# Down projection's token operands split one unit behind their activations, stored as high and low halves; weight buffers shared by two products; accumulators loaded ahead

## The chip, the cores and the metric

The kernel runs on one core of a Trainium2 chip. A core has five engines that run side by side, each with its own queue of instructions: PE (TensorE, the matrix engine; its weight loads are a row of their own, PEld), DVE (VectorE), ACT (ScalarE), POOL (GpSimd) and SP (SyncE). Here SP issues all the DMAs that this text speaks of, one after the other. The engines' operands lie in SBUF (128 partitions); matmuls add up in banks of PSUM (the kernel has eight, named m).

The metric is the time of one execution in device microseconds. The kernel before took 2537.41 us, the median of three runs (2534.61 to 2539.2).

## The reference

One step of a streaming encoder with a single layer, in fp32: 512 new frames of one stream with 16 learned tokens ahead of them, and 64 frames of another stream with a cache.

```python
def trunk_layer(x, ...):
    h = rmsnorm(x, norm_attn_g)
    ...                                    # projections, two kinds of attention
    x = x + mix @ w_out
    h = rmsnorm(x, norm_ffn_g)
    x = x + (silu(h @ ffn_w_gate) * (h @ ffn_w_up)) @ ffn_w_down
    return x, ...
y_prompt = rmsnorm(xp[:, N_META:], final_norm_g)
y_sample = rmsnorm(xs, final_norm_g)
```

The width D_MODEL is 2048 and the FFN's width D_FF is 5632. In the FFN the kernel holds 576 tokens (TQ = 576, in two halves of QH = 288).

## The kernel before

**fp32 out of three matmuls.** Every fp32 operand is split into a high half, an ACT copy rounded to fp32r, and a low half, the DVE subtraction of that from the source. A product is then three matmuls: high x high, high x low, low x high. For weights the halves are wh and wl, for tokens bh and bl.

**Seven products instead of eight.** The FFN works on 2 x 2 blocks. `winograd` (L1068 to L1134) runs over seven products p; the token side of a product is one of seven combinations of four quarters (11, 12, 21, 22), the weight side one of seven combinations of raw weight blocks. Weight combinations are sums (ws) made on POOL (L1095) or DVE. For each product it splits the weights (`split_weights`), runs 2n matmuls with wh (L1126) and n with wl (L1130), each 128x128 by 128x288, and hands the bank to `take`, which copies (ACT) or adds (DVE) it into the result. Then it calls `step()`, by which other work is put behind that product in program order.

**Gate and up projection** (L1280 to L1329, about 1000 to 1962 us). 22 units u, each a gate set ("g") and an up set ("u") of seven products with n = 8, so 24 matmuls a product. Raw weights (raw, 1 MB each) come in by DMA. `gated` (L1268) multiplies the gate result by the token norm and applies silu; then POOL multiplies the up result by it (L1315) and forms four sums of quarters (L1321 to L1324) in the gate result's buffer. The results c go to HBM as actspill (two stores a unit), the sums as sumspill.

**Down projection** (L1426 to L1455, about 1970 to 2447 us). The 22 units of activations are taken in blocks of [4, 4, 4, 4, 4, 2]. Five blocks run `down_rows` (L1358): for each of eight pairs of output column blocks d, one `winograd` with n = 4, that is 7 x 12 matmuls, added into the accumulators y0 to y15 by DVE. Token operands of the next block are built meanwhile: `builder` (L1228) loads a quarter or a sum from actspill or sumspill (144 KB) four ahead, and a call of `step` issues half of its split (bh on ACT, bl on DVE, in place). For the first block this starts behind the third product of the last up set. In all 148 operands are split like this. wh and wl have two buffers each. The accumulators start as the residual and are loaded (x2spill) a pair at a time during the first block.

**Last block** (L1338, L1372 to L1424). Two units remain; `plain_rows` multiplies them without the seven products (L205), per half of the tokens, `squares` sums up for the norm, and `finish` transposes on PE (L1394), scales into output tiles (ot, four buffers) and stores.

**What sets the order.** Instructions go through a scheduler that orders each engine's queue; PE runs in program order, `pin` (from the down projection on) keeps the split in program order, and Q is the queue of loads and stores on SP. A new pool of buffers can be used once the buffers of the one that lay there are done: the pools of the gate and up stage are closed, and yy and yp opened, ahead of the down projection.

```python
    CHAIN = ((1, "a"), (5, "b"), (6, "a"), (2, "c"), (7, "a"), (3, "b"), (4, "a"))
    WIDE = ((1, "a"), (2, "c"), (4, "d"), (5, "b"), (6, "a"), (3, "b"), (7, "a"))
```

These are the orders of the products with their banks: CHAIN in the down projection and the last up set, WIDE elsewhere.

Of the kernel before, what the change touches and what calls it, by code (L numbers as in the profile page):

```python
# [2 lines left out]

# [128 lines left out]
def encoder_step(  # L132
# [196 lines left out]
    sumspill = dp.tile([FC // 2, P, 4, QH], F32, name="sumspill")  # L329
    mspill = dp.tile([KC, P, TQ], F32, name="mspill")  # L330
# [673 lines left out]
    rb2 = rw.tile([P, TQ], F32, name="rb2")  # L1004
    sq2 = rw.tile([P, TQ], F32, name="sq2")
# [13 lines left out]

    def operand(m, p, src):  # L1020
        hi = bc.tile([P, QH], F32R, name=f"bh{p}_{m}")
        lo = bc.tile([P, QH], F32R, name=f"bl{p}_{m}")
        pin(S.activation(hi, src, AF.Copy))
        pin(V.tensor_tensor(lo, src, f32(hi), op=ALU.subtract))
        operands[m, p] = (hi, lo)
# [41 lines left out]

    def winograd(wpool, spool, raws, slots, take, banks=None, engine=V, step=lambda: None, stag=("ws", 3),  # L1068
# [117 lines left out]
    close_ma()  # L1186
    fb, close_fb = pool("fb", "right")


    def stile():  # L1190
        return fr.tile([P, QH], F32, name="s", tag="s", bufs=4)

    def combined(c11, c12, c21, c22, chain):
# [15 lines left out]
        def take(p, banks):  # L1209
            if p == 1:  # L1210
                s[1] = stile()
                S.activation(s[1], banks[1], AF.Copy)
            elif p == 6:
                s[2] = stile()
# [13 lines left out]
    def builder(m0, count, plain, ahead, by_product=False):  # L1228

        srcs = {}  # L1230
        for m in range(m0, m0 + count):
            quarter = [actspill[2 * m + f, :, c] for f in range(2) for c in (slice(0, QH), slice(QH, TQ))]
            if plain:
                for p, src in zip((1, 2, 4, 5), quarter):
                    srcs[m, p] = src
            else:
                for p, src in zip(ORDER, (quarter[0], quarter[2], sumspill[m, :, 2], sumspill[m, :, 0],
                                          sumspill[m, :, 1], quarter[3], sumspill[m, :, 3])):
                    srcs[m, p] = src
        order = [p for p, _ in CHAIN]  # L1240
        todo = sorted(srcs, key=lambda mp: order.index(mp[1])) if by_product else list(srcs)

        def fetch(n):
            for m, p in todo[n:n + 1]:
                hi = bc.tile([P, QH], F32R, name=f"bh{p}_{m % 8}")
                lo = bc.tile([P, QH], F32R, name=f"bl{p}_{m % 8}")
                load(f32(lo), srcs[m, p])
                operands[m % 8, p] = (hi, lo)

        for n in range(ahead):  # L1250
            fetch(n)
        for n, (m, p) in enumerate(todo):
            fetch(n + ahead)
            hi, lo = operands[m % 8, p]
            pin(S.activation(hi, f32(lo), AF.Copy))
            yield
            pin(V.tensor_tensor(lo, f32(lo), f32(hi), op=ALU.subtract))
            yield
# [17 lines left out]

    turn = 0
    norm = token_norm()
    start = builder(0, blocks[0], False, 4, True)
    for u in range(FC // 2):  # L1280
        out = {}
        for which, wsrc in (("g", w_gate), ("u", w_up)):
# [9 lines left out]
            take = combined(*quarters(c[:, 0, :], c[:, 1, :]), chain)  # L1292
            done = [0]

            def step():
                if u == 0 and which == "u":
                    next(norm, None)
                if u == FC // 2 - 1 and which == "u":
                    done[0] += 1
                    if done[0] > 2:  # L1300
                        for _ in range(2 * blocks[0]):
                            next(start, None)
# [23 lines left out]
    for _ in start:  # L1326
        pass
# [206 lines left out]
```

## Time and profile before

| what | us |
|---|---|
| median of 3 runs | 2537.41 (2534.61 to 2539.2) |
| the profiled execution | 2533.22 |
| its span in the trace | 2531.3 |
| PE busy in the span | 2440.7 (96%) |
| DVE busy in the span | 1800.2 (71%) |
| ACT, POOL busy | 1106.6 (44%), 744.3 (29%) |

The span runs from the first to the last instruction of one profiled execution; 1.9 us of that execution lie outside it. In the rows of groups of instructions, `out<-in` names the tiles, `x824` is the count, then follow busy us, mean ns of one, and the engine's idle us ahead of them with what ended it. A busy PE is not PE at full rate: matmuls are pipelined, so the number of matmuls in a stretch says more than the busy share. A row of the windows has the stretch, then busy us and count for PE, PEld, DVE, ACT and POOL, then the clock that TensorE was granted, the DMA engines' busy share, and GB/s. A row of the timeline has start and length in us, with the idle time ahead in brackets. From the page of before:

```profile
PE   8999999989999999999999999999999899999997
...
DVE  5555555556555568877777777777777899999975
```

These are the busy tenths in 40 slices of 63.3 us: DVE's busiest stretch are the slices of the down projection, 32 to 38.

### The profile page before, as it was taken

Reading aid. Unit: us, or ns where it says so; the run is one execution under the profiler, and the core shown is the slowest. Engines: PE = TensorE matmul, PEld = TensorE weight load, DVE = VectorE, ACT = ScalarE, POOL = GpSimd, SP = SyncE. Lnnn points to the kernel's source line nnn. Section 1 sums busy time; section 2 is a strip of 40 time slices with the busy share of each in tenths; the row PEclk is TensorE's granted clock in tenths of the full one; section 3 lists DMA queues with packets and bytes.
Section 4 is the critical chain, followed back from the end, with each engine's and each line's share of the span. In section 5 each row is a group of like instructions: output and inputs, shape, how many; then the busy total and the mean of one; then the engine's idle time right before and its main releaser. Section 6 shows DMA issues by size and latency. Waiting matters only on the chain. (4 is left out here: it accounts for less than half of the span.)

```text
span 2531.3 us, 44872 instructions
## 1 busy us (share of the span) xinstructions
PE 2440.7 (96%) x17847; PEld 2381.8 (94%) x17847; DVE 1800.2 (71%) x2826; ACT 1106.6 (44%) x2008; POOL 744.3 (29%) x621
## 2 busy tenths in 40 slices
PE   8999999989999999999999999999999899999997
PEld 6999999988999888999999999999999899999997
DVE  5555555556555568877777777777777899999975
ACT  5343333333433444444444444444445444444445
POOL 0000000010000265644545454454543222222236
PEclk9999999999999999999999999999999899999999
DMA  7432232334322553333433333333335642542334
GB/s 216 141 93 80 81 87 83 82 111 120 100 84 76 166 151 112 125 126 121 137 109 117 117 125 132 119 125 100 128 128 167 207 150 84 159 157 84 111 100 150
DMA packets 330116, 307.73 MB, mean 122 GB/s; under 512 B 24708, under 2 KB 298507, under 8 KB 329907
## 3 DMA queue, kind: packets, MB, share of 16 engines
q1 hardware_dynamic: 329346, 302.80, 38.3%
q8 instruction: 140, 2.29, 0.4%
q0 software_dynamic: 560, 2.06, 0.2%
q14 instruction: 70, 0.57, 0.1%
HBM read 250.82 MB, written 56.68 MB: 121 GB/s over the span
## 5 line engine op out<-in xcount | busy, mean ns | idle before, releaser
L1126 PE MATMUL m<-bh,wh 128*128 128x288 f32 x3584 | 968.0, 296 | 11.0 <-DMA bl<-sumspill 8.4
L1126 PE MATMUL m<-bl,wh 128*128 128x288 f32 x3584 | 967.5, 295 | 0.0
L1126 PEld LDWEIGHTS m<-bh,wh 128*128 128x128 f32 x3584 | 673.9, 188 | 11.8 <-ACT wh L125 11.7
L1126 PEld LDWEIGHTS m<-bl,wh 128*128 128x128 f32 x3584 | 677.4, 189 | 0.1
L1130 PE MATMUL m<-bh,wl 128*128 128x288 f32 x3584 | 585.5, 298 | 17.1 <-DVE wl L125 14.5
L1130 PEld LDWEIGHTS m<-bh,wl 128*128 128x128 f32 x3584 | 512.2, 188 | 30.6 <-DVE wl L125 30.1
L1095 POOL TENSOR_TENSOR ws<-raw 128x512 f32<-128x512 f32 x256 | 344.1, 1352 | 599.1 <-DVE wl L125 319.2
L125 ACT ACTIVATE wh<-ws 128x512 fp32r<-128x512 f32 (+1 forms) x340 | 288.8, 849 | 447.6 <-PE m L1126 296.8
L125 DVE TENSOR_TENSOR wl<-ws,wh 128x512 fp32r<-128x512 f32 (+1 forms) x340 | 378.8, 1114 | 114.3 <-ACT wh L125 114.3
L125 DVE TENSOR_TENSOR wl<-raw,wh 128x512 fp32r<-128x512 f32 x416 | 403.7, 984 | 26.1 <-ACT wh L125 16.8
L125 ACT ACTIVATE wh<-raw 128x512 fp32r<-128x512 f32 x416 | 249.7, 626 | 306.2 <-PE m L1126 279.9
L108 PE MATMUL ps<-xh,wh 128*128 128x296 f32 x960 | 221.4, 312 | 1.2 <-ACT wh L125 1.2
L108 PE MATMUL ps<-xh,wl 128*128 128x296 f32 x960 | 210.7, 301 | 1.2 <-DVE wl L125 1.2
L108 PE MATMUL ps<-xl,wh 128*128 128x296 f32 x960 | 210.5, 301 | 0.0
L108 PEld LDWEIGHTS ps<-xh,wh 128*128 128x128 f32 x960 | 157.1, 191 | 5.5 <-ACT wh L125 1.7
L108 PEld LDWEIGHTS ps<-xh,wl 128*128 128x128 f32 x960 | 157.0, 190 | 2.2 <-DVE wl L125 2.2
L125 DVE TENSOR_TENSOR y<-y,m 128x288 f32<-128x288 f32 x312 | 139.6, 447 | 27.2 <-PE m L1130 18.0
L108 PEld LDWEIGHTS ps<-xl,wh 128*128 128x128 f32 x960 | 157.5, 190 | 0.0
L125 DVE TENSOR_TENSOR ws<-ws,raw 128x512 f32<-128x512 f32 x128 | 92.3, 722 | 83.6 <-POOL ws L1095 77.2
L125 DVE TENSOR_TENSOR wl<-wr,wh 128x1024 fp32r<-128x1024 f32 (+1 forms) x110 | 117.7, 1070 | 36.9 <-ACT wh L125 35.4
L125 ACT ACTIVATE wh<-wr 128x1024 fp32r<-128x1024 f32 (+1 forms) x110 | 101.7, 929 | 61.8 <-PE ps L108 52.0
L1273 POOL TENSOR_TENSOR c<-c,rb 128x576 f32<-128x576 f32 x44 | 73.2, 1664 | 164.8 <-ACT c L125 162.3
(359 smaller groups left out, 3342.5 us busy)
## 6 DMA issues: line engine op xcount, KB each, us to landing
raw<-in_ffn_w_gate SPq DMA_DIRECT2D x44, 1024.0 KB, 6.9
raw<-in_ffn_w_up SPq DMA_DIRECT2D x44, 1024.0 KB, 5.9
raw<-in_ffn_w_down SPq DMA_DIRECT2D x40, 1024.0 KB, 5.4
wr<-in_w_in SPq DMA_DIRECT2D x60, 512.0 KB, 4.0
actspill<-c SPq DMA_DIRECT2D x44, 288.0 KB, 2.1
sumspill<-c SPq DMA_DIRECT2D x20, 576.0 KB, 2.8
bl<-sumspill SPq DMA_DIRECT2D x80, 144.0 KB, 3.5
bl<-actspill SPq DMA_DIRECT2D x68, 144.0 KB, 3.9
```

What stands on the lines that cost most here:

```text
L108: self.tc.keep_in_program_order(self.pe.matmul(out, lhsT, rhs, start=start, stop=stop))
L125: ins = issue(*args, **kwargs)
L1095: engine.tensor_tensor(w[:, k:k + m, :], pick(xs), pick(ys), op=op)
L1126: PE.matmul(banks[p], wh[:, k, :], x, start=first and new and k == 0 and x is hi, stop=False, skip_group_check=not new)
L1130: PE.matmul(banks[p], wl[:, k, :], hi, start=False, stop=last and k == n - 1, skip_group_check=not new)
L1273: G.tensor_tensor(g[:, f, :], g[:, f, :], rb2, op=ALU.mult)
```

## The change

**Splits.** In units 2 to 19 the seven token operands of the down projection are split during the next unit: `parts` is a generator that is advanced behind steps 5 to 7 of its gate set and 1 to 4 of its up set. Each piece is a one-column ACT copy of that step's product, the ACT copy to the high half, the DVE subtraction, and one store of both halves to partspill (288 KB). In the down phase `fetch_parts` loads both halves at once and nothing is left to split. The first two units (WHOLE = 2) and the last block's two are still stored in actspill and sumspill and split on arrival, 22 operands in all; actspill is stored for four units instead of 22 and sumspill for two instead of 20.

**Weights.** wh and wl have two buffers of eight blocks; two products of n = 4 share one (`weight_tiles`).

**Turn to the down projection.** `starter` fetches the first block's operands one product at a time behind the seven products of the last up set and splits those of two units. There the gating multiply stands on POOL by quarters, and SP's queue keeps program order (`Q.ordered`) until the second column pair of the first block. Pools fs and fw stay open. Accumulators y0 and y1 take the norm's buffers, y2 to y4 a raw buffer; y5 to y15 are loaded ahead of the second column pair. Sums, norm values and output tiles at the end take operand buffers that are done (`room`), so output tiles no longer take turns in four.

```diff
+    partspill = dp.tile([FC // 2, P, 8, 2, QH], F32, name="partspill")
...
+    def weight_tiles(wpool, n):
+        if n == 8 or not spare:
+            both = [wpool.tile([P, 8, P], F32R, name=x, tag=x, bufs=2) for x in ("wh", "wl")]
+            if n == 8:
+                return both
+            spare.append([w[:, 4:8, :] for w in both])
+            return [w[:, 0:4, :] for w in both]
+        return spare.pop()
...
-            wh = wpool.tile([P, n, P], F32R, name="wh", tag="wh", bufs=2)
-            wl = wpool.tile([P, n, P], F32R, name="wl", tag="wl", bufs=2)
+            wh, wl = weight_tiles(wpool, n)
...
+    PIECE = {1: 0, 2: 2, 3: 3, 5: 4, 6: 5, 4: 6, 7: 7}
+    def fetch_parts(m, p):
+        load(f32(operand_tile(m % 8, p)), partspill[m, :, PIECE[p]])
+    def fetcher(m0, count):
+        n = 0
         for m in range(m0, m0 + count):
+            for p in ORDER:
+                fetch_parts(m, p)
+                yield
+                n += 1
+                if n % 2 == 0:
+                    yield
...
+    def starter():
...
+        todo = [p for p, _ in CHAIN]
+        for i in range(len(todo) + 2):
+            if i < len(todo):
+                for m in range(blocks[0]):
+                    if m < WHOLE:
+                        fetch_whole(m, todo[i], whole(m, todo[i]))
+                    else:
+                        fetch_parts(m, todo[i])
+            if i > 1:
+                for m in range(WHOLE):
+                    split_in_place(m, todo[i - 2])
+            yield
...
+    def parts(u, srcs):
+        for p in ORDER:
+            b = fb.tile([P, 2, QH], F32R, name="parts", tag="parts", bufs=2)
+            S.activation(b[:, 0, 0:1], (yield), AF.Copy)
+            S.activation(b[:, 0, :], srcs[PIECE[p]], AF.Copy)
+            V.tensor_tensor(b[:, 1, :], srcs[PIECE[p]], f32(b[:, 0, :]), op=ALU.subtract)
+            store(partspill[u, :, PIECE[p]], f32(b))
+        yield
...
+            if ending:
+                Q.ordered = True
+                fetch_raw(0, blocks[0], 0)
+                accumulator(0, rw.tile([P, TQ], F32, name="y0", tag="rows", bufs=2))
...
+                    if p in (2, 7, 3, 4):
+                        q = {2: 0, 3: 1, 4: 2, 7: 3}[p]
+                        G.tensor_tensor(w[q], w[q], g[q], op=ALU.mult)
...
+                if pieces and (which == "u" or done[0] > 4):
+                    try:
+                        pieces.send(took[WIDE[done[0] - 1][0]][:, 0:1])
...
-            if u < FC // 2 - 1:
+            if u < WHOLE or FC // 2 - blocks[-1] <= u < FC // 2 - 1:
                 store(actspill[2 * u + f], w[:, f, :])
...
-            store(sumspill[u], t)
+            if u < WHOLE:
+                store(sumspill[u], t)
+            else:
+                pieces = parts(u, [b11, b12, b21, b22] + [t[:, i, :] for i in range(4)])
...
+    fetch_raw(0, blocks[0], 1)
+    y234 = rw.tile([P, 8 * 256], F32, name="y234", tag="raw", bufs=1)
+    for i in range(2, 5):
+        accumulator(i, y234[:, (i - 2) * TQ:(i - 1) * TQ])
     for f in range(2):
         store(actspill[FC - 2 + f], out["u"][:, f, :])
-    close_fb()
-    close_rw()
-    yy, close_yy = pool("yy", "right")
-    close_fw()
-    yp, close_yp = pool("yp")
...
-            ot = yp.tile([P, 512], F32, name="ot", tag="ot", bufs=OT_BUFS)
+            ot = room(others)[:, 0:512]
...
             for d in range(KC // 2):
-                if bi == 0:
-                    for i in (2 * d, 2 * d + 1):
-                        y.append(yy.tile([P, TQ], F32, name=f"y{i}"))
-                        load(y[i], x2spill[i])
+                if bi == 0 and d == 1:
+                    Q.ordered = False
+                    close_fb()
+                    yy, close_yy = pool("yy", "right")
...
+                    for i in range(6, KC):
+                        accumulator(i, yy.tile([P, TQ], F32, name=f"y{i}"))
+                if (first, d) not in fetched:
+                    fetch_raw(first, n, d)
                 down_rows(first, n, d, slots, step)
```

SP's queue in the first block of the down projection, where the raw weights of the third column pair are fetched (raw from in_ffn_w_down; y accumulators from x2spill, bl operands from actspill and sumspill). Before:

```order
L125 DMA y8_22271<-x2spill_68 128x576
L125 DMA y9_22273<-x2spill_68 128x576
L125 DMA bl6_6_22296<-sumspill_70 128x288
L125 DMA bl3_6_22340<-actspill_69 128x288
L125 DMA bl7_6_22382<-sumspill_70 128x288
L125 DMA bl1_7_22423<-actspill_69 128x288
L125 DMA raw_21968<-in_ffn_w_down 128x8x256
L125 DMA y10_22426<-x2spill_68 128x576
L125 DMA y11_22428<-x2spill_68 128x576
```

And the same fetch with the change (raw_22396; b operands of both halves from partspill):

```order
L125 DMA y11_22254<-x2spill_68 128x576
L125 DMA y12_22256<-x2spill_68 128x576
L125 DMA y13_22258<-x2spill_68 128x576
L125 DMA y14_22260<-x2spill_68 128x576
L125 DMA y15_22262<-x2spill_68 128x576
L125 DMA b3_4_22280<-partspill_71 128x576
L125 DMA b2_5_22377<-partspill_71 128x576
L125 DMA b4_5_22394<-partspill_71 128x576
L125 DMA raw_22396<-in_ffn_w_down 128x8x256
L125 DMA b5_5_22434<-partspill_71 128x576
```

The raw fetch now stands behind all accumulators; before, y10 to y15 came after it.

DVE's queue in the steady down loop (ws sums of weights, y accumulators, bl operands of the next block). Before:

```order
L125 TENSOR_TENSOR y6_22119<-y6_22119,m_24533 128x288
L125 TENSOR_TENSOR bl5_5_24359<-bl5_5_24359,bh5_5_24358 128x288
L125 TENSOR_TENSOR wl_24579<-ws_24576,wh_24578 128x512
L125 TENSOR_TENSOR y7_22121<-y7_22121,m_24552 128x288
L125 TENSOR_TENSOR wl_24598<-raw_24531,wh_24597 128x512
L125 TENSOR_TENSOR y6_22119<-y6_22119,m_24533 128x288
L125 TENSOR_TENSOR bl6_5_24401<-bl6_5_24401,bh6_5_24400 128x288
L125 TENSOR_TENSOR wl_24621<-ws_24618,wh_24620 128x512
```

With the change:

```order
L125 TENSOR_TENSOR y6_22244<-y6_22244,m_24644 128x288
L125 TENSOR_TENSOR wl_24703<-raw_24642,wh_24702 128x512
L125 TENSOR_TENSOR wl_24703<-ws_24721,wh_24702 128x512
L125 TENSOR_TENSOR y7_22246<-y7_22246,m_24662 128x288
L125 TENSOR_TENSOR ws_24816<-ws_24799,raw_24776 128x512
L125 TENSOR_TENSOR y6_22244<-y6_22244,m_24644 128x288
L125 TENSOR_TENSOR wl_24743<-ws_24740,wh_24742 128x512
L125 TENSOR_TENSOR wl_24743<-raw_24642,wh_24742 128x512
```

The bl rows are gone, and two wl rows in a row write into one buffer (wl_24703, then wl_24743).

ACT's queue behind a gate set, at the turn to the up set (m the product's bank, c results, parts the split slices). Before:

```order
L125 ACTIVATE c_15788<-m_15789 128x288
L125 ACTIVATE wh_16027<-raw_16021 128x512
L125 ACTIVATE wh_16027<-raw_16023 128x512
L125 ACTIVATE c_15788<-c_15788 128x576
L125 ACTIVATE wh_16059<-raw_16021 128x512
```

With the change:

```order
L125 ACTIVATE c_14925<-m_14926 128x288
L125 ACTIVATE parts_14920<-c_14925 128x1
L125 ACTIVATE parts_14920<-c_14668 128x288
L125 ACTIVATE wh_15179<-raw_15173 128x512
L125 ACTIVATE wh_15179<-raw_15175 128x512
L125 ACTIVATE parts_15091<-c_14925 128x1
L125 ACTIVATE parts_15091<-c_14668 128x288
L125 ACTIVATE c_14925<-c_14925 128x576
L125 ACTIVATE wh_15216<-raw_15173 128x512
L125 ACTIVATE wh_15216<-raw_15175 128x512
L125 ACTIVATE parts_15128<-c_14925 128x1
L125 ACTIVATE parts_15128<-c_14416 128x288
```

Each copy of a slice now stands behind a one-column copy that reads the result of the current step (c_14925), and both stand ahead of the next weight copies.

More of the change, by code (lines that the diff above doesn't have):

```diff
@@ L1 @@
+import itertools
 import math
@@ L1226, in combined @@
         return take
-    def builder(m0, count, plain, ahead, by_product=False):
-        srcs = {}
-        for m in range(m0, m0 + count):
[L1232 to L1248, printed above, removed]
-        for n in range(ahead):
[L1251 to L1255, printed above, removed]
@@ new lines, in fetch_whole, with act_quarter, whole @@
+    def fetch_whole(m, p, src):
+        operand_tile(m % 8, p)
+        load(f32(operands[m % 8, p][1]), src)
+    def act_quarter(m, q):
+        return actspill[2 * m + q // 2, :, q % 2 * QH:(q % 2 + 1) * QH]
+    def starter():
+        def whole(m, p):
+            q = PIECE[p]
+            return act_quarter(m, q) if q < 4 else sumspill[m, :, q - 4]
+        todo = [p for p, _ in CHAIN]
[10 more added lines that the diff above has]
+            yield
@@ L1256, in builder @@
+    def builder(m0, count, ahead):
+        todo = [(m, p, act_quarter(m, q)) for m in range(m0, m0 + count) for q, p in enumerate((1, 2, 4, 5))]
+        for n in range(ahead):
+            fetch_whole(*todo[n])
+        for n, (m, p, _) in enumerate(todo):
+            if n + ahead < len(todo):
+                fetch_whole(*todo[n + ahead])
             yield
-            pin(V.tensor_tensor(lo, f32(lo), f32(hi), op=ALU.subtract))
+            split_in_place(m % 8, p)
             yield
@@ L1275, in encoder_step, with fetch_raw, accumulator @@
     blocks = [4, 4, 4, 4, 4, 2]
+    WHOLE = 2
+    def parts(u, srcs):
[6 more added lines that the diff above has]
+        yield
+    fetched = {}
+    def fetch_raw(m0, n, d):
+        fetched[m0, d] = load_raw(fr, w_down, m0 * 256, 2 * n, d * 256, 2)
+    y = {}
+    def accumulator(i, tile):
+        y[i] = halves(tile)
+        load(tile, x2spill[i])
     turn = 0
     norm = token_norm()
-    start = builder(0, blocks[0], False, 4, True)
+    start = starter()
+    pieces = None
     for u in range(FC // 2):
@@ L1365, in take, with room @@
                 V.tensor_tensor(c, c, banks[p], op=ALU.add)
-        winograd(yp, yp, raws, slots, take, step=step, chain=CHAIN)
+        winograd(fw, fs, raws, slots, take, step=step, chain=CHAIN)
     tok = [[(0, NS), (NS, P), (192, 96)], [(QH, P), (416, P), (544, 32)]]
     sqs = {}
+    def room(names):
+        return bc.tile([P, 2, QH], F32, name=next(names)).rearrange("p a b -> p (a b)")
     def squares(i, h):
-        c = y[i][:, h * QH:(h + 1) * QH]
+        c = y[i][h]
         if i == 0:
-            sqs[h] = stile()
+            sqs[h] = room(others)[:, 0:QH]
             G.tensor_tensor(sqs[h], c, c, op=ALU.mult)
         else:
-            t = stile()
+            t = room(sums)[:, 0:QH]
             G.tensor_tensor(t, c, c, op=ALU.mult)
@@ L1430, in encoder_step @@
         if bi + 1 < len(blocks):
-            build = builder(first + n, blocks[bi + 1], bi + 2 == len(blocks), 4)
+            if bi + 2 == len(blocks):
+                build = builder(first + n, blocks[bi + 1], 4)
+            else:
+                build = fetcher(first + n, blocks[bi + 1])
             def step():
@@ L1444, in encoder_step @@
         else:
+            rest = [m for m in range(8) if m not in slots]
+            sums = itertools.cycle([f"b{p}_{rest[-1]}" for p in ORDER])
+            others = iter([f"b{p}_{m}" for m in rest[-2::-1] for p in ORDER])
             before = iter(())
```

76 lines of the change are left out of this document (50 added, 26 removed).

## Prediction

> **What bounds the kernel now.** The page comes first, with its busy times; then the busy time by stage, from the windows, and when DVE's operand splits run (ns of the fastest, the median and the longest, then the first and the last start).
>
> ```profile
> span 2531.3 us, 44872 instructions
> PE 2440.7 (96%) x17847; PEld 2381.8 (94%) x17847; DVE 1800.2 (71%) x2826; ACT 1106.6 (44%) x2008; POOL 744.3 (29%) x621
> ...
> core 0: us, PE busy (x) PEld busy (x) DVE busy (x) ACT busy (x) POOL busy (x), PEclk, DMA share, GB/s
> 1010.00:1925.00 915.00, 913.36 (x6863) 912.90 (x6863) 687.22 (x779) 400.38 (x615) 458.60 (x328) 1.00 0.36 122
> 2000.00:2350.00 350.00, 337.94 (x2465) 328.25 (x2465) 324.24 (x572) 164.09 (x308) 77.75 (x59) 1.00 0.40 127
> 2385.00:2446.00 61.00, 60.87 (x458) 60.55 (x457) 52.69 (x87) 24.03 (x38) 12.90 (x10) 1.00 0.26 79
> 2446.00:2514.00 68.00, 62.28 (x449) 58.25 (x449) 44.15 (x78) 39.17 (x71) 52.86 (x60) 1.00 0.50 149
> ...
> L125 DVE TENSOR_TENSOR bl<-bl,bh x148: 442/451/1682, 1945.3 to 2383.5; 128x288 fp32r<-128x288 f32 x148
> ```
>
> PE is busy everywhere, so I count matmuls per us instead of busy time. Gate and up projections: 6863 / 915 = 7.50 per us, 0.1333 us each, with DVE at 75%. Down projection: 2465 / 350 = 7.04, DVE at 93%. The last operand split starts at 2383.5; from 2385 on the same loop runs at 458 / 61 = 7.51 with DVE at 86%. So the down projection is short of full rate while DVE also splits operands. Who holds PE up there, and DVE's work, by groups (window 2000 to 2350):
>
> ```profile
> L1130 PE MATMUL m<-bh,wl 128*128 128x288 f32 x824 | 148.9, 302 | 12.1 <-DVE wl L125 10.0
> ...
> L125 DVE TENSOR_TENSOR y<-y,m 128x288 f32<-128x288 f32 x206 | 92.1, 447 | 8.7 <-PE m L1130 7.7
> L125 DVE TENSOR_TENSOR wl<-ws,wh 128x512 fp32r<-128x512 f32 x117 | 87.2, 745 | 0.0
> L125 DVE TENSOR_TENSOR wl<-raw,wh 128x512 fp32r<-128x512 f32 x88 | 75.2, 854 | 0.0
> L125 DVE TENSOR_TENSOR bl<-bl,bh 128x288 fp32r<-128x288 f32 x103 | 67.8, 658 | 0.0
> L125 DVE TENSOR_TENSOR ws<-ws,raw 128x512 f32<-128x512 f32 x29 | 20.1, 692 | 16.0 <-POOL ws L1095 14.3
> ```
>
> PE waits for DVE's low weight halves (wl). The operand splits (bl) are 67.8 of DVE's 324 us. The other loss lies between up and down projection; PE's timeline there, and where the plain rows (L205) start:
>
> ```profile
> 1960.78 1.23 PE L1130 MATMUL m<-bh,wl 128*128 128x288 f32 x8
> 1970.45 0.61 PE L1126 MATMUL m<-bh,wh 128*128 128x288 f32 x1 [8.43 <-DMA bl<-sumspill]
> ...
> 1973.63 1.33 PE L1130 MATMUL m<-bh,wl 128*128 128x288 f32 x4 [0.89 <-DVE wl L125]
> ...
> 1977.63 0.41 PE L1126 MATMUL m<-bh,wh 128*128 128x288 f32 x1
> ...
> 2447.16 0.29 PE L205 MATMUL m<-bh,wh 128*128 128x288 f32 x1
> ```
>
> The up projection ends at 1960.78 + 8 x 0.1333 = 1961.85. From there to 2447.16 are 485.3 us for 5 x 8 x 7 x 12 = 3360 matmuls, which take 448.0 at full rate: 37.3 us lost. Of these 8.6 are idle, 4.0 go in the first 24 matmuls (to 1977.63: 7.18 us instead of 3.2, half speed and a 0.9 us wait for wl), and 24.7 in the other 3336 (469.5 us instead of 444.8).
>
> **Part 1: 126 splits move from the down to the gate/up stage.** This adds 7 per unit in 18 units, each an ACT copy, a DVE subtraction, a 288 KB store and a one-column ACT copy behind that step's product. I cost them at nothing. At the turn from gate to up projection, where two gating multiplies stand too, the timeline of before has the rows below; with them a short ACT copy from the finish, the operand copies as a group, and PE's group of wl matmuls in gate/up (1010 to 1925):
>
> ```profile
> 1577.78 1.15 ACT L125 ACTIVATE wh<-raw 128x512 fp32r<-128x512 f32 x2 [1.71 <-PE m L1126]
> 1580.97 0.69 ACT L125 ACTIVATE c<-c 128x576 f32<-128x576 f32 x1 [2.03 <-DVE c L125]
> ...
> 1584.31 0.68 DVE L125 TENSOR_TENSOR wl<-raw,wh 128x512 fp32r<-128x512 f32 x1
> ...
> 2517.75 0.20 ACT L125 ACTIVATE rc<-vc 128x3 f32<-128x3 f32 x1 [0.93 <-DVE vc L125]
> ...
> L125 ACT ACTIVATE bh<-bl 128x288 fp32r<-128x288 f32 x148 | 62.9, 431 | 10.7 <-DMA bl<-sumspill 7.6 <-DMA bl<-actspill 1.5 <-PE m L1126 0.9
> ...
> L1130 PE MATMUL m<-bh,wl 128*128 128x288 f32 x2288 | 353.8, 296 | 1.6 <-DVE wl L125 1.5
> ```
>
> The one-column copy is bounded by nothing and by the 0.69 of the 576-wide one; I take the 0.20 of three columns. With 0.43 for the copy behind it (62.9 us for 148) ACT gets 0.63 us per step of 3.2, where it idles 1.7 to 2 us. While ACT waits there for a product, the next weight copy (wh) is queued behind it, and PE waits for that; but the copy's own product ends 3.2 us before wh is due. On DVE the tightest row is the wl that ends at 1584.99. The first up product starts about 1582.4, the second 1585.6, and its wl matmuls 16 x 0.1333 later, at 1587.7: 2.7 us to spare. Ahead of it come three added subtractions, 3 x 0.45 = 1.35 us from the median, 3 x 0.66 = 2.0 from the mean above. It still fits. Without this cover the price would be up to 126 x 0.658 = 83 us. SP's queue: a store now stands ahead of raw loads, later by 1 to 2 us, for raws that are read 20 us later.
>
> **Part 2: the down loop.** Blocks 1 to 4 only load operands; DVE per pair of column blocks loses 3.5 x 0.658 = 2.3 us of 11.9. Weight buffers become eight wide and hold two products each, so a wl may be written two products (3.2 us) ahead, not one. Both point to the rate seen after the last split, 7.51, and to 7.50 as in gate/up; I take a little less, 7.47, for the longer loads. Loads per pair grow from 1.05 + 0.52 to 1.05 + 1.38 MB: 8.1 us of 11.2 at the 301 GB/s below. They fit.
>
> **Part 3: the turn.** Operands of the first block are now fetched behind each of the seven products, two units of four still split on arrival, and pools stay open, so the first pair of column blocks starts at once at 1961.85 and two pairs run to 1961.85 + 22.4 = 1984.25. But on SP's queue the raw weights of the third pair stand behind everything else. From 1961.85 on: last operands 0.88, raw of the second pair 1.05, y2 to y4 0.88, activations 0.59, five operands 1.47, y5 to y15 3.24, three operands 0.88, then the raw itself 1.05: 10.06 MB. The rates are from these rows:
>
> ```profile
> 1988.00:1996.00 8.00, 8.00 (x63) 8.00 (x62) 7.34 (x14) 4.16 (x8) 2.59 (x2) 1.00 1.07 385
> 1956.00:1960.00 4.00, 4.00 (x33) 4.00 (x32) 3.99 (x10) 2.77 (x7) 0.00 (x0) 1.00 1.00 301
> ...
> raw<-in_ffn_w_down SPq DMA_DIRECT2D x3, 1024.0 KB, 5.4
> actspill<-c SPq DMA_DIRECT2D x44, 288.0 KB, 2.1
> ```
>
> 10.06 MB take 26.1 us at 385 (rows of y, 2304 bytes a partition) and 33.4 at 301 (operand rows of 1152 bytes). Most of it is of the first kind: I take 27.5, and 1.6 for landing (2.1 less its transfer): 1991.0. With wh 0.6 us later PE restarts at about 1991.8: idle 7.5 us, between 5.5 and 14. The clock then costs what it cost before. Granted clock in the same place:
>
> ```profile
> 1962.00:1970.00 8.00, 0.02 (x1) 0.00 (x0) 4.22 (x8) 2.23 (x6) 2.30 (x3) 0.64 0.92 307
> 1970.00:1978.00 8.00, 6.66 (x26) 6.32 (x27) 4.83 (x7) 2.95 (x6) 3.70 (x3) 0.51 0.90 288
> ```
>
> 8 us idle, then 26 matmuls in 8 us at 0.51: 7.18 - 3.2 - 0.9 of waiting = 3.1 us. [...]
>
> **The sum.** Between 1961.85 and the plain rows: lost before 37.3; after 7.5 idle + 3.1 clock + 3192 / 7.47 - 425.6 = 1.7, together 12.3. Gain 25.0. Plain rows and finish, as the transposes' group (2446 to 2514) and the waits (total us, times, longest), with PE's wait in the first gate/up unit (850 to 1010) last:
>
> ```profile
> L1394 PE MATMUL m<-ident,y 128*128 128x128 f32 (+2 forms) x49 | 6.5, 273 | 0.0
> ...
> PE m L205 <- DVE wl L125: 3.0, 8, 0.7
> PE m L205 <- ACT wh L125: 1.9, 3, 1.4
> ...
> DVE ot L125 <- DMA out<-ot: 3.6, 4, 1.6
> ...
> PE m L1126 <- ACT wh L125: 2.6, 2, 1.8
> ```
>
> The 68 us from 2446 hold 384 matmuls (51.2 us) and 49 transposes (6.5): some 10 lost, of which 4.9 are waits for weights that the deeper buffers ease. I take 4, between 0 and 9. Output tiles no longer take turns in four buffers: 1.5 us, between 0 and 3.6. The first unit's products, now in paired buffers too, I put at 0, between -2 and 2 (PE waits 2.6 for wh there). Sum 25.0 + 4 + 1.5 = 30.5. The profiled execution took 2533.2 (span 2531.3), so 2502.7; the runs shown have a median of 2537.4, 4.2 above it, so **2506 us** there, rounded.
>
> **Rivals.**
> - *The third pair's raw weights are not late* (a transfer hidden anyway). For it: 385 GB/s was held for 8 us. Against: the bytes alone need 26 us of 22.4. PE would save 7.5 + 3.1: 2495.5. [...] Chance 0.10.
> - *The down loop stays short of PE.* DVE's mean for wl from raw is 854 ns, of which only the neighbours' work, not the splits, may be the cause, and operand bytes double, so that raws land later. If a third of 24.7 comes back instead of nearly all: 16 us less gain, 2522. For it: POOL's subtractions stay in place. Against: 7.51 after the last split with POOL still at it. Chance 0.17.
> - *The moved splits delay PE in gate/up.* The place is the wl of the second up product. It costs from the point where DVE is over 2.7 us later there, and cancels the gain at 2.7 + 30.5 / 18 = 4.4 us. Contended subtractions and ACT waiting for a late sum would have to come together. At 2 us a unit: 2506 + 36 = 2542, slower. For it: DVE goes from 75% to some 83%. Against: PE waits 1.5 us for wl in those 915 us. Chance 0.07.
> - *It does not do what it says*: the loss only moves from the split to the loads, and the turn idles 14 us and more, the loop gaining little: 2535. Chance 0.05.
>
> **How the numbers follow.** Forecast 0.61, at 2506, own range 2499 to 2516 (idle 5.5 to 14, plain rows 0 to 9). With the first two rivals 0.88 lie between 2494 and 2524. A measurement of this kernel tells some 0.2% (5 us) from no change: faster 0.88, same 0.05, slower 0.07.
>
> **What would show it.** Right: gate/up windows still at 7.50 per us; no idle PE at 1962, but one wait of 5 to 14 us some 22 us later, for wh behind a raw load, and a half clock after it; then 7.4 or more to the plain rows, DVE at 80 to 88%. Wrong: waits for wl or wh spread over gate/up; a down rate near 7.04; no wait at the third pair.

## The result and the profile after

The changed kernel took 2516.2 us, the median of four runs (2515.51 to 2518.8), beside 2538.3 us (2534.61 to 2539.68) for the kernel before: a ratio of 0.9917, with a 95% interval of 0.99 to 0.9934. It is faster by some 21 us. That lies in the range of the prediction (2494 to 2524), 0.2 us past the end of the forecast's own range (2499 to 2516); the forecast was 2506. The profiled execution took 2515.51 us. From the page of after:

```profile
span 2513.7 us, 45128 instructions
PE 2434.5 (97%) x17847; PEld 2385.2 (95%) x17847; DVE 1791.5 (71%) x2826; ACT 1126.1 (45%) x2134; POOL 758.5 (30%) x623
```

DVE and PE are about as busy as before. The count of matmuls per us shows the change. The windows of after (stretch; busy us and count of PE, PEld, DVE, ACT, POOL; clock; DMA share; GB/s):

```profile
1010.00:1925.00 915.00, 912.99 (x6847) 912.25 (x6846) 746.21 (x903) 479.23 (x867) 466.08 (x328) 1.00 0.41 139
2000.00:2350.00 350.00, 349.33 (x2610) 348.10 (x2611) 288.20 (x503) 127.19 (x224) 91.17 (x62) 1.00 0.55 180
2005.00:2425.00 420.00, 419.37 (x3150) 418.13 (x3149) 345.70 (x609) 154.21 (x270) 108.05 (x73) 1.00 0.49 161
```

Gate and up projection still run at 6847 / 915 = 7.48 per us with 124 more operations on DVE. The down projection runs at 2610 / 350 = 7.46, and from 2005 us on at 3150 / 420 = 7.50, PE's full rate. What is lost, is lost ahead of that. PE's timeline of after (start, length, then in brackets the idle time ahead and what ended it):

```profile
1963.43 1.24 PE L1147 MATMUL m<-b,wl 128*128 128x288 f32 x8
...
1968.62 1.30 PE L1143 MATMUL m<-b,wh 128*128 128x288 f32 x8 [0.78 <-DVE y L125]
...
1978.27 1.60 PE L1143 MATMUL m<-b,wh 128*128 128x288 f32 x8 [3.03 <-DVE y L125]
1979.67 1.17 PE L1147 MATMUL m<-b,wl 128*128 128x288 f32 x4
1980.63 2.06 PE L1143 MATMUL m<-b,wh 128*128 128x288 f32 x8
...
1996.94 2.29 PE L1143 MATMUL m<-b,wh 128*128 128x288 f32 x8 [4.16 <-ACT wh L125]
2000.04 1.33 PE L1147 MATMUL m<-b,wl 128*128 128x288 f32 x4 [0.80 <-DVE wl L125]
...
2426.27 0.43 PE L205 MATMUL m<-b,wh 128*128 128x288 f32 x2
```

The up projection ends at 1963.43 + 8 x 0.1333 = 1964.50, the plain rows start at 2426.27. That splits the span (us):

| stage | before | after | after less before | forecast |
|---|---|---|---|---|
| to the end of the up projection | 1961.85 | 1964.50 | +2.65 | 0 |
| five blocks of the down projection | 485.3 | 461.8 | -23.5 | -25.0 |
| plain rows and finish | 84.1 | 87.4 | +3.3 | -5.5 |
| span | 2531.3 | 2513.7 | -17.6 | -30.5 |

Of the first row, 1.5 us were there when the FFN's first product started (972.18 against 970.63 us), ahead of the code that was changed. In after and ten of the twelve kernels of the next section, which differ from it by at most one fetch up to there, the up projection ends between 1961.60 and 1965.79 us; so the 2.65 isn't shown to be a cost of the change. The medians differ by 22.1 us and not by 17.6, since the profiled execution of before (2533.22) was faster than each of its four timed runs.

**The wait at 1978 us was not forecast.** PE waits for an accumulation into y, which frees its bank. Timelines of POOL and DVE in after:

```profile
1974.71 2.50 POOL L1112 TENSOR_TENSOR ws<-raw 128x512 f32<-128x512 f32 x2 [8.12 <-DMA raw<-in_ffn_w_down]
...
1976.02 1.74 DVE L125 TENSOR_TENSOR ws<-ws,raw 128x512 f32<-128x512 f32 x1 [2.87 <-POOL ws L1112]
1977.68 0.44 DVE L125 TENSOR_TENSOR y<-y,m 128x288 f32<-128x288 f32 x1
```

The raw weights of the second pair, fetched behind the last operands, land at 1974.6. POOL sums them, DVE's next sum waits for POOL, and an accumulation is queued behind that sum on DVE.

**The plain rows and the finish got slower.** ACT's timeline of before, then of after, over one period and the start of the next:

```profile
2460.67 0.54 ACT L125 ACTIVATE y<-y,gT 128x288 f32<-128x288 f32 x1 [1.46 <-POOL s L1379]
2461.11 0.62 ACT L125 ACTIVATE wh<-raw 128x512 fp32r<-128x512 f32 x1
2462.18 0.54 ACT L125 ACTIVATE y<-y,gT 128x288 f32<-128x288 f32 x1 [0.46 <-POOL s L1379]
2462.62 0.61 ACT L125 ACTIVATE wh<-raw 128x512 fp32r<-128x512 f32 x1
```

```profile
2446.91 0.54 ACT L125 ACTIVATE y<-y,gT 128x288 f32<-128x288 f32 x1 [2.33 <-POOL b L1480]
2447.35 1.14 ACT L125 ACTIVATE wh<-raw 128x512 fp32r<-128x512 f32 x2
...
2451.29 0.54 ACT L125 ACTIVATE y<-y,gT 128x288 f32<-128x288 f32 x1 [2.33 <-POOL b L1480]
```

The period for 24 matmuls is 2451.29 - 2446.91 = 4.38 us; 3.2 is full rate (24 x 0.1333). In before one wh copy stood behind each scaling of y; in after a scaling that waits for POOL's square stands ahead of two. PE of before in the same place has the period 2462.76 - 2458.95 = 3.81:

```profile
2458.95 0.40 PE L205 MATMUL m<-bh,wl 128*128 128x288 f32 x1 [0.20 <-DVE wl L125]
...
2462.76 0.40 PE L205 MATMUL m<-bh,wl 128*128 128x288 f32 x1 [0.39 <-DVE wl L125]
```

The period is not the whole of the 3.3 us. Both kernels have 240 matmuls from the start of the plain rows to PE's first matmul for the norm (`ones`), and take 38.6 us for them before and 38.95 after. With the change PE's first wait comes 14.0 us into the plain rows instead of 4.2, and the longer periods behind it take that gain back. The other 2.9 us lie behind that point: after waits 1.57, 1.29 and 1.45 us for the norm's sums, before 0.44 us for them and 1.44 for a weight copy.

### The profile page after: what moved, and what is told of

Same layout as the page of the kernel before. It is cut to its first block, busy times and chain, and to the rows that moved or that the text cites. A ratio compares the mean times of both kernels' runs of the same rounds, so it can differ in the third digit from the quotient of the medians.

```text
span 2513.7 us, 45128 instructions
## 1 busy us (share of the span) xinstructions
PE 2434.5 (97%) x17847; PEld 2385.2 (95%) x17847; DVE 1791.5 (71%) x2826; ACT 1126.1 (45%) x2134; POOL 758.5 (30%) x623
## 4 chain that ended last, share of the span: by engine, by line
PE 49%; DVE 2%; DMA 1%; POOL 1%; issue 1%; ACT 1%; POOLq 0%; DVEq 0%; ACTq 0%
PE m L1143 32%; PE m L1147 16%; DVE wl L125 1%; DMA raw<-in_ffn_w_down 1%; POOL b L1480 0%; ACT wh L125 0%; DVE y L125 0%; DVE b L125 0%; DVE ws L125 0%; PE m L1495 0%; ACT L125 0%; POOL ws L1112 0%; POOL b L1481 0%; ACT b L125 0%; PE m L205 0%
## 5 line engine op out<-in xcount | busy, mean ns | idle before, releaser
L1143 PE MATMUL m<-b,wh 128*128 128x288 f32 x7168 | 1051.1, 296 | 11.2 <-ACT wh L125 6.8
L1143 PEld LDWEIGHTS m<-b,wh 128*128 128x128 f32 x7168 | 986.9, 189 | 13.8 <-ACT wh L125 7.5
L1147 PE MATMUL m<-b,wl 128*128 128x288 f32 x3584 | 580.7, 297 | 3.1 <-DVE wl L125 3.0
L1112 POOL TENSOR_TENSOR ws<-raw 128x512 f32<-128x512 f32 x256 | 366.3, 1440 | 558.4 <-DVE wl L125 260.4
L1147 PEld LDWEIGHTS m<-b,wl 128*128 128x128 f32 x3584 | 514.3, 189 | 5.0 <-DVE wl L125 4.9
L125 DVE TENSOR_TENSOR wl<-ws,wh 128x512 fp32r<-128x512 f32 (+1 forms) x340 | 391.1, 1161 | 91.8 <-ACT wh L125 91.4
L125 DVE TENSOR_TENSOR wl<-raw,wh 128x512 fp32r<-128x512 f32 x416 | 384.8, 950 | 25.7 <-ACT wh L125 24.9
L125 DVE TENSOR_TENSOR ws<-ws,raw 128x512 f32<-128x512 f32 x128 | 115.2, 903 | 74.9 <-POOL ws L1112 72.8
L1412 POOL TENSOR_TENSOR c<-c 128x576 f32<-128x576 f32 x42 | 73.8, 1757 | 85.6 <-DVE c L125 81.7
```

Of the source, the lines that this page charges most:

```text
L125: ins = issue(*args, **kwargs)
L1112: engine.tensor_tensor(w[:, k:k + m, :], pick(xs), pick(ys), op=op)
L1143: PE.matmul(banks[p], wh[:, k, :], x, start=first and new and k == 0 and x is hi, stop=False, skip_group_check=not new)
L1147: PE.matmul(banks[p], wl[:, k, :], hi, start=False, stop=last and k == n - 1, skip_group_check=not new)
L1412: G.tensor_tensor(w[:, f, :], w[:, f, :], g[:, f, :], op=ALU.mult)
```

## The experiments

Twelve kernels, each timed in turns with the kernel before on its chip. "Against before" is the ratio; the changed kernel's is 0.9917, and 0.001 is 2.5 us. The stages are those of the table above.

| run | median us | against before (95%) | down blocks | plain rows and finish |
|---|---|---|---|---|
| changed kernel | 2516.2 | 0.9917 (0.99 to 0.9934) | 461.8 | 87.4 |
| raw3_first | 2510.18 | 0.9899 (0.9886 to 0.9913) | 455.1 | 87.8 |
| turn_order | 2503.03 | 0.9872 (0.9858 to 0.9885) | 451.3 | 87.1 |
| rows_own | 2513.43 | 0.9912 (0.9899 to 0.9926) | 462.9 | 82.8 |
| late_scaling | 2513.64 | 0.9919 (0.9905 to 0.9932) | 461.7 | 87.5 |
| late_pinned | 2525.42 | 0.9956 (0.9942 to 0.9969) | 463.3 | 97.0 |
| scaled_apart | 2507.14 | 0.9884 (0.987 to 0.9897) | 461.6 | 80.2 |
| loop_unpaired | 2523.44 | 0.9945 (0.9933 to 0.9958) | 469.1 | 88.9 |
| before_paired | 2561.69 | 1.0101 (1.0087 to 1.0115) | see text | 126.7 |
| no_column | 2552.36 | 1.006 (1.0047 to 1.0073) | | |
| turn_and_apart | 2497.89 | 0.9846 (0.9832 to 0.9859) | 451.8 | 80.3 |
| turn_apart_own | 2499.57 | 0.985 (0.9837 to 0.9864) | | 79.9 |
| act_squares | 2495.84 | 0.9834 (0.9821 to 0.9848) | 452.7 | 77.4 |

### The turn: order or bandwidth

```diff
                     close_fb()
+                    fetch_raw(first, n, 2)
                     yy, close_yy = pool("yy", "right")
...
                     for i in range(6, KC):
                         accumulator(i, yy.tile([P, TQ], F32, name=f"y{i}"))
+                    Q.ordered = False
```

> The changed kernel, with the raw weights of the third column pair fetched ahead of y5 to y15 instead of behind them; nothing else. Theory (order on SP's queue): the changed kernel's wait at the third pair (4.2 us for wh, 0.8 us for wl, and the half clock behind it) goes, the 3.0 us wait at the second pair stays: 5 to 7 us faster than the changed kernel (about 2510 against 2516), first matmul of the third pair at once behind the second pair. Rival (the DMA engines are full from 1956 to 2000 us at 352 GB/s, whatever stands first): the wait moves to an accumulator or the fourth pair, gain below 2 us.

The five blocks took 455.1 us, 6.7 less than in the changed kernel. PE's timeline of this run, around the second and third pair:

```profile
1979.35 1.30 PE L1143 MATMUL m<-b,wh 128*128 128x288 f32 x8 [2.58 <-DVE y L125]
2003.65 1.32 PE L1143 MATMUL m<-b,wh 128*128 128x288 f32 x8 [0.16 <-ACT wh L125]
2006.83 0.79 PE L1147 MATMUL m<-b,wl 128*128 128x288 f32 x4 [1.85 <-DVE wl L125]
```

The wait of 4.16 us is gone, the one at the second pair stays, and a wait of 1.85 us appears at the fourth pair, which is a little of what the rival said. By the totals the gain over the changed kernel is 4.6 us (0.9899 against 0.9917), with intervals that overlap. The next kernel also changes what stands ahead of the second pair:

```diff
                 if ending:
+                    if done[0] == 7:
+                        fetch_raw(0, blocks[0], 1)
                     next(start)
...
-    fetch_raw(0, blocks[0], 1)
...
-                down_rows(first, n, d, slots, step)
+                down_rows(first, n, d, slots, step if bi or d else lambda: None)
```

> As raw3_first, and the raw weights of the second pair ahead of the last product's operands, and no operands of the next block fetched during the first column pair. Theory (order): the down projection's five blocks, 461.8 us in the changed kernel against 448.0 at full rate, come within 3 us of full rate: 10 to 13 us faster than the changed kernel (about 2504). Rival (bandwidth): at least 4 us of idle PE stay between 1964 and 2005 us, gain below 6 us.

451.3 us, 10.5 less, and 3.3 from full rate. PE's longest wait between the up projection and 2012 us is now 1.14 us, at the second pair (3.03 before this edit). Which of the two new edits shortened it wasn't tried apart. The windows of after, then of turn_order, from 1956 to 2004:

```profile
1956.00:2004.00 48.00, 39.23 (x262) 38.24 (x261) 32.31 (x54) 15.77 (x31) 11.73 (x10) 0.89 1.01 348
```

```profile
1956.00:2004.00 48.00, 45.52 (x340) 44.87 (x339) 39.17 (x67) 20.07 (x39) 13.42 (x11) 1.00 1.02 356
```

Both keep the DMA engines full (busy shares of 1.01 and 1.02), at 348 and 356 GB/s; one gets 262 matmuls done in it, the other 340. So the turn is bound by the order of the transfers, not by their sum: what is needed later was moved ahead of what was needed next.

### The plain rows: shared buffers, queue order or POOL

Here the plain rows take one of the two weight buffers for each split, as before.

```diff
-                wh, wl = weight_tiles(fw, 4)
+                wh, wl = [w[:, 0:4, :] for w in weight_tiles(fw, 8)]
```

> The changed kernel, with weight buffers of the last block's plain rows no longer shared by two products (each split takes one of the two buffers for itself, as in the kernel before). Theory (sharing reorders ACT's queue, a y scaling that waits for POOL ahead of both wh copies): 24 matmuls of the plain rows go from 4.38 us back to about 3.85 us, and the kernel is 4 to 8 us faster than the changed kernel. Rival (the sums' and output tiles' new buffers slow the plain rows): 4.38 us stays, no change.

The period goes back to 3.85 us and the stage to 82.8 us, 4.6 less than in the changed kernel. PE's timeline of rows_own:

```profile
2443.32 0.40 PE L205 MATMUL m<-b,wl 128*128 128x288 f32 x1 [0.41 <-DVE wl L125]
2447.17 0.40 PE L205 MATMUL m<-b,wl 128*128 128x288 f32 x1 [0.41 <-DVE wl L125]
```

In the runs that leave the plain rows as they are in after (raw3_first, turn_order, late_scaling, loop_unpaired) that stage took 87.1 to 88.9 us. Of the 4.6 us, 1.2 lie ahead of the norm's first matmul and 3.4 behind it, where the waits for the norm's sums are down to one of 0.44 us. The total moved less than expected, within its interval (0.9912 against 0.9917), because the blocks ahead took 1.1 us more and the stretch before them 0.6 us. So sharing costs here, by one of two ways: through ACT's order, or because two buffers come free only behind two products each. Two edits tried to move the scaling back:

```diff
-        S.activation(c, c, AF.Copy, scale=gE[:, i:i + 1])
+        late.append((i, c))
+        if len(late) > 2:
+            scale_late()
```

> The changed kernel with shared weight buffers, but the ACT scaling of an accumulator (squares) issued two calls later. Theory (ACT's queue order is what costs, not the buffers): 24 matmuls of the plain rows take 3.9 us or less instead of 4.38, 5 to 12 us faster than the changed kernel; the floor is POOL's four operations for a pair, 0.67 + 1.12 + 0.67 + 0.81 = 3.27 us. Rival (two buffers released only behind two products are what costs): 4.38 us stays.

Nothing moved. But ACT's timeline of late_scaling shows that the edit didn't reach the queue: the scheduler had put the scaling where it stood in the changed kernel.

```profile
2444.93 0.54 ACT L125 ACTIVATE y<-y,gT 128x288 f32<-128x288 f32 x1 [2.33 <-POOL b L1480]
2445.37 1.13 ACT L125 ACTIVATE wh<-raw 128x512 fp32r<-128x512 f32 x2
```

So this run doesn't tell the two ways apart. The next one also holds ACT in program order in the last block (`S.ordered = True`):

> As late_scaling, and ACT's queue in the last block held in program order, so that the scaling really stands behind the next weight copies (in late_scaling the scheduler put it back where it was). Theory (a scaling that waits for POOL ahead of the wh copies is what costs): 24 matmuls of the plain rows take 3.3 to 3.9 us instead of 4.38, 5 to 14 us faster than the changed kernel. Rival (the buffers shared by two products are what costs): 4.38 us stays.

```profile
2447.11 0.54 ACT L125 ACTIVATE y<-y,gT 128x288 f32<-128x288 f32 x1 [2.33 <-POOL b L1480]
2447.56 1.13 ACT L125 ACTIVATE wh<-raw 128x512 fp32r<-128x512 f32 x2
```

The period stays at 4.38: one pair later is not late enough, a scaling that waits for POOL still stands ahead of the next copies. The second half got slower, since the finish's ACT work is then held in program order too (waits of 3.26 and 2.52 us for wh, 97.0 us for the stage), and the kernel 9 to 10 us slower than the changed one. The clean test leaves queue order and buffers as they are and takes away what the scaling waits for. It writes to a buffer of its own, so POOL need not have read the unscaled values first:

```diff
-        S.activation(c, c, AF.Copy, scale=gE[:, i:i + 1])
+        if i % 2 == 0:
+            scaled[i // 2, h] = room(others)
+        z = halves(scaled[i // 2, h])[i % 2]
+        S.activation(z, c, AF.Copy, scale=gE[:, i:i + 1])
```

> The changed kernel, with ACT's scaling of an accumulator written to another buffer (a finished operand tile) instead of in place, so that it no longer waits for POOL's square of the unscaled values; ACT's order stays, and output tiles take turns in 13 buffers. Theory (a scaling that waits for POOL stands ahead of the next wh copies): 24 matmuls of the plain rows go from 4.38 us to 3.3 to 3.8 us, limited by POOL's 3.27 us at the least, and the kernel is 6 to 14 us faster than the changed kernel. Rival (two buffers that are shared by two products are released too late): 4.38 us stays, no change.

ACT's timeline of scaled_apart:

```profile
2443.54 0.54 ACT L125 ACTIVATE b<-y,gT 128x288 f32<-128x288 f32 x1 [1.77 <-DVE y L125]
2443.99 1.14 ACT L125 ACTIVATE wh<-raw 128x512 fp32r<-128x512 f32 x2
...
2447.35 0.54 ACT L125 ACTIVATE b<-y,gT 128x288 f32<-128x288 f32 x1 [1.80 <-DVE y L125]
```

With the same order and shared buffers the period is 2447.35 - 2443.54 = 3.81 us, and the stage 80.2 us, 7.2 less: 3.5 us ahead of the norm's first matmul and 3.7 behind it, where PE also no longer falls to half clock (0.51 from 2470.5 to 2474.0 us in after; the longest wl matmul of the plain rows took 0.44 us there and 0.40 here). The edit also gives the output tiles 13 buffers in turn, which wasn't tried apart; the first 3.5 us lie ahead of any output tile. The scaling's wait for POOL was the price; that the buffers are shared is not, by itself. POOL is now without a gap there, 0.67 + 0.81 + 1.11 + 1.14 = 3.73 us a period. So half of the squares were moved from POOL to ACT, on top of turn_and_apart:

```diff
-            G.tensor_tensor(t, c, c, op=ALU.mult)
+            if i % 2:
+                S.activation(t, c, AF.Square)
+            else:
+                G.tensor_tensor(t, c, c, op=ALU.mult)
```

> turn_and_apart, with every second square of the plain rows made by ACT instead of POOL. Theory (POOL bounds the plain rows once the scaling no longer waits for it: 0.67 + 0.81 + 1.11 + 1.14 = 3.73 us of a period of 3.81): POOL's work per period falls to some 2.6 us and the period to 3.2 to 3.5 us, 4 to 9 us faster than turn_and_apart (2489 to 2494). Rival (the loop from wl through PE and the accumulator's addition back to ACT bounds it): 3.8 us stays, within 2 us.

PE no longer waits for weights: the 240 matmuls up to the norm's first take 31.99 us, which is full rate, 3.4 less than in turn_and_apart. But the stage is only 2.9 us shorter (77.4 against 80.3), and the total 2 to 3 us (0.9834 against 0.9846, intervals that overlap), less than the 4 to 9 expected. POOL did bound the first stretch. The part behind it got 0.6 us longer: two waits for the norm there are followed by 14 matmuls at 0.24 us each, which turn_and_apart hasn't.

### The loop: splits or shared buffers

Two kernels make, with before and after, all four combinations. In the first the five blocks of the changed kernel take one buffer for each product. In the second the kernel before shares them, with the splits still in the loop; its output tiles have one buffer instead of four to make room, so only its loop is read.

```diff
-        if n == 8 or not spare:
+        if n == 8 or not spare or not pair[0]:
...
+            if not pair[0]:
+                return [w[:, 0:4, :] for w in both]
```

> The changed kernel, with weight buffers of the five down-projection blocks that are not shared by two products: each product takes one of the two buffers for itself. Theory (the removed splits alone bring the loop to full rate; before, 7.51 matmuls per us were seen behind the last split with unshared buffers): from 2005 us to the plain rows still 7.45 to 7.50 per us, within 4 us of the changed kernel. Rival (sharing is what lets the low weight halves be ready): the rate falls to 7.0 to 7.3, 10 to 28 us slower than the changed kernel.

> The kernel before, with weight buffers of the down projection shared by two products as in the change (the splits stay in the loop; output tiles get one buffer instead of four, which makes room and lengthens the finish by some us). Theory (the splits hold DVE): 2000 to 2350 us stays at 7.0 to 7.15 matmuls per us. Rival (sharing does it): 7.35 or more, some 15 us faster between 2000 and 2447 us.

The windows from 2010 to 2350 of before, loop_unpaired, before_paired and after, in this order:

```profile
2010.00:2350.00 340.00, 328.07 (x2393) 318.66 (x2393) 314.56 (x555) 159.29 (x299) 75.16 (x57) 1.00 0.41 129
```

```profile
2010.00:2350.00 340.00, 337.70 (x2510) 333.61 (x2509) 293.58 (x480) 132.87 (x211) 80.28 (x60) 1.00 0.53 175
```

```profile
2010.00:2350.00 340.00, 335.84 (x2493) 331.48 (x2492) 316.49 (x578) 154.41 (x311) 86.73 (x60) 1.00 0.43 133
```

```profile
2010.00:2350.00 340.00, 339.37 (x2547) 338.13 (x2547) 279.87 (x489) 124.49 (x219) 88.59 (x60) 1.00 0.55 180
```

7.04, 7.38, 7.33 and 7.49 matmuls per us. Neither theory held alone: each half of the change brings back two thirds (sharing) to three quarters (the moved splits) of the lost rate by itself, and both together nearly all of it. In us, from PE's restart to the plain rows, before_paired took 2432.84 - 1972.48 = 460.4 where before took 476.7: 16.3 of the 24.7 us that were lost there. loop_unpaired's blocks took 469.1, 7.3 more than after's. With shared buffers DVE may stay at 93% (316.49 of 340 us in before_paired) and PE loses little: its waits for wl, 10.0 us of this window in before, are gone from the list of its waits. That the halves are ready earlier is the likely reason; it wasn't measured by itself.

### The one-column copies

```diff
-            S.activation(b[:, 0, 0:1], (yield), AF.Copy)
+            yield
```

> The changed kernel without the one-column copies; the seven slices of a unit are then free to stand in ACT's queue as soon as they fit. Theory (the copies only keep a slice that waits for POOL's sums from standing ahead of the weight copies): PE gets waits for wh or wl in gate and up projection, 0.5 to 2 us a unit, 9 to 36 us slower than the changed kernel. Rival (the copies are not needed): gate and up projection stay at 7.50 per us, within 3 us.

Slower by 36 us than the changed kernel, at the upper end of what was expected. The windows and ACT's waits (total us, times, longest) of no_column from 1010 to 1925:

```profile
1010.00:1925.00 915.00, 889.88 (x6600) 878.98 (x6599) 765.47 (x869) 418.18 (x717) 472.01 (x319) 1.00 0.40 134
...
ACT parts L125 <- POOL c L1412: 111.0, 36, 4.0
ACT parts L125 <- DMA partspill<-parts: 64.1, 38, 3.6
ACT parts L125 <- POOL c L1420: 34.7, 18, 1.9
```

Gate and up projection fall to 7.21 per us. Without the copy as an anchor the slices stand in ACT's queue right behind the unit, ahead of the next weight copies, and wait there for POOL's gating multiply, its sums, and their own two buffers. In the changed kernel ACT's slices wait for POOL nowhere in this window, and once for their buffers, 0.2 us. The group of parts copies on ACT in after, one-column and whole ones together:

```profile
L125 ACT ACTIVATE parts<-c 128x1 fp32r<-128x1 f32 x252 | 81.4, 323 | 34.3 <-DVE c L125 28.4 <-DMA partspill<-parts 0.2
```

81.4 us for 126 pairs are 0.65 a pair. Less the whole copy (0.43 us by the operand copies of before, 0.445 by the median of no_column), the one-column copy takes 0.20 to 0.22 us.

### Together

> turn_order and scaled_apart together. The two places lie apart in time, so the gains should add up: 10 us for the turn and that of scaled_apart, 2490 to 2498 us. If they share a cause (SP's queue), less.

2497.89 us. The gains add up within a fraction of a us by stage (451.8 and 80.3 us, where each alone had 451.3 and 80.2).

> As turn_and_apart, and the plain rows' weight buffers not shared by two products. If the scaling's wait was all that sharing cost, the same time as turn_and_apart within 2 us; if sharing has a price of its own there, 2 to 5 us faster.

The same within the intervals: with the scaling's wait gone, sharing has no further price in the plain rows. The fastest versions, turn_and_apart and act_squares, beat the changed kernel by some 18 to 21 us, as much again as the change itself.

## Why the prediction was right, and where it was off

- **Part 1 (moved splits cost nothing in gate and up projection): right.** The window has 7.48 per us, and PE's only wait there was 1.87 us at 1022 us, in a place where before has 1.49. The one-column copy was taken at 0.20 us and measured 0.20 to 0.22. The margin at the turn was smaller than the 2.7 us of the prediction: PE's timeline of before has the first two up products start at 1581.85 and 1585.04 us and the wl matmuls in question at 1587.16, which leaves 2.2; the 1.35 to 2.0 us of added subtractions still fit. That ACT idles long enough holds only where the copy holds the slice back: no_column prices that cover at 36 us.
- **Part 2 (7.47 per us in the loop): right in size, for a reason that was half read.** The loop reached 7.46 to 7.50. The prediction took the splits' absence and the shared buffers as two reasons that each point to full rate, with the 7.51 behind the last split of before as witness. The four windows show that each alone gives 7.33 to 7.38. The 7.51 was a poor witness: loop_unpaired has no splits there either and yet runs at 7.38 up to 2350, and only in its last 48 us at full rate. What sets that last stretch apart wasn't tried and stays open.
- **Part 3 (the turn, 7.5 us idle and 3.1 of clock at the third pair): right in sum, in part by luck, and spread otherwise.** The idle time was 0.78 + 3.03 + 4.16 + 0.80 = 8.8 us, and the five blocks lost 13.8 us in all where 12.3 were forecast. The half clock came behind two waits and not one (granted 0.50 from 1979.6 to 1982.5 and from 1997 to 2002 us). The 20 matmuls behind each took 4.26 and, without the wait of 0.80, 5.30 us instead of 2.67, some 4.2 us lost where 3.1 were forecast; against that, the 1.7 us set down for the rest of the loop didn't come (7.50 per us from 2005 us on). The forecast has two pairs run through without a wait, to 1984.25; it counted the second pair's raw weights among the bytes ahead of the third's, but not that they land too late for their own pair. raw3_first takes the third pair's wait away and turn_order shortens the second's from 3.03 to 1.14 us, by what SP issues when.
- **The sum's term for plain rows and finish: wrong in sign.** The prediction took 4 us of gain "between 0 and 9" for plain rows and 1.5 for the finish, since deeper buffers ease waits for weights. Measured: 3.3 us of loss. The mistake is the step from "4.9 are waits for weights" to the buffers. They did ease the start (PE's first wait 14.0 us in, not 4.2). But the steady waits came from a scaling in ACT's queue that waited for POOL, and sharing put it ahead of two weight copies instead of one; that took the gain back and made the norm's sums late. rows_own (no sharing there) takes 4.6 us off, scaled_apart (no such wait) 7.2. As for output tiles, DVE's and ACT's waits for them (3.6 and 2.0 us in before) are gone, but from the last matmul of the plain rows to the end it took 19.2 us against 17.9. The 8.8 us from 5.5 of gain to 3.3 of loss are most of what the forecast was too low by; 1.5 are the turn, and 2.65 the stretch ahead, of which 1.5 lie before the changed code.
- **Two sums of the prediction are off by 1 us.** 2502.7 + 4.2 is 2506.9 and not 2506, and a third of the 24.7 us instead of the 23.0 in the sum is 14.8 us less gain and not 16.
- **Rivals.** The down loop did not stay short, the moved splits did not delay PE, and the raw weights were late, for two pairs. The fourth, that it does not do what it says, fell too: the loss did not move to the loads.

## What to carry to other kernels

Here a buffer shared by two products also made one unit of them in the queues: what waited 1.46 or 0.46 us ahead of one copy of 0.62 us now waits 2.33 us ahead of two that take 1.14. So look at what stands between the copies, not only at how early a buffer is free. Where a transfer phase fills the DMA engines anyway, put each transfer where its first reader needs it; about the same bytes (348 and 356 GB/s) gave 262 or 340 matmuls in 48 us. And look at what reads the source of an instruction that overwrites it in place: the scaling waited 2.33 us for POOL's square of the same values, and giving it a buffer of its own took 7 us off a stage that moving the instruction by one pair could not.

## What the runs showed of the hardware

**A wl subtraction on DVE that started during a POOL sum ended 0.54 to 0.56 us behind it.** DVE's timeline of before:

```profile
2030.35 1.70 DVE L125 TENSOR_TENSOR wl<-raw,wh 128x512 fp32r<-128x512 f32 x1
...
2032.71 0.68 DVE L125 TENSOR_TENSOR wl<-raw,wh 128x512 fp32r<-128x512 f32 x1
```

POOL's timeline of before has one sum from 2030.22 to 2031.51:

```profile
2030.22 1.29 POOL L1095 TENSOR_TENSOR ws<-raw 128x512 f32<-128x512 f32 x1 [2.81 <-DVE wl L125]
```

The same operation takes 0.68 us alone and 1.70 when it starts during the sum. From 2000 to 2350 us of before, the 174 subtractions for wl that touch no sum took 0.67 to 0.69 us, and 6 during which a sum started took no longer. The 25 that started during a sum took 1.30 to 1.79, and each ended 0.54 to 0.56 us behind the sum's end. The mean of 854 ns in the prediction's second rival is a mix of the two.

**Waits of 3.03 and 2.57 us were followed by half clock, one of 2.58 us was not.** In after the rows at 1979.67 and 1980.63 above take 0.24 us a matmul (four in 0.96 us), behind an idle time of 3.03 us; the granted clock is 0.66 from 1978 to 1983 us, and 0.50 from 1979.6 to 1982.5. In rows_own a wait of 2.57 us was followed by the same (0.60 from 1979 to 1983), in raw3_first one of 2.58 us was not (1.00 in the same window): the eight matmuls behind the one took 2.25 us, behind the other 1.30. PE's timelines of these two:

```profile
1978.76 2.25 PE L1143 MATMUL m<-b,wh 128*128 128x288 f32 x8 [2.57 <-DVE y L125]
```

```profile
1979.35 1.30 PE L1143 MATMUL m<-b,wh 128*128 128x288 f32 x8 [2.58 <-DVE y L125]
```

Two shorter waits close together were followed by it too: in after 1.57 and 1.29 us at the norm, with 18 matmuls in the 5.3 us from 2465.2 on, by 0.51 from 2470.5 to 2474.0, and in act_squares 0.59 and 0.85 us by 0.56 from 2451.5 to 2455.4. In scaled_apart 1.35 and 0.68 us were not (1.00). The longest wl matmul of the plain rows took 0.44 us in after and act_squares, 0.40 in scaled_apart. What decides it, these runs don't settle.
